# The two query tiles as one pair job ahead of the xg pair jobs, and wv tiles split by GpSimd with an accumulating DMA, in a one-core hybrid layer

## The chip, the cores and the metric

The kernel runs on 1 core of one Trainium2 chip (trn2). The metric is device time in microseconds (us), the median of several runs. The engines are named as in the profile: PE is TensorE's matmul and PEld its weight load, DVE is VectorE, ACT ScalarE, POOL GpSimd, SP SyncE, which here only issues DMAs.

## The reference

One layer of a streaming encoder, batch 1, 512 tokens (SEQ), width 1024 (D): a SwiGLU block, a mixing block, and a second SwiGLU block, each between two RMS norms. All is float32. The change lies in the mixing block:

```
u = pre_mix(h)
q, k, v, xr, xg = split(u @ w_in)            # 1024, 256, 256, 1024, 1024 columns
hr  = rg_lru(causal_conv(xr))                # gated linear recurrence over the tokens
y_a = (hr * gelu(xg)) @ w_lru_out
y_b = sliding_window_attention(q, k, v) @ w_attn_out     # 16 query heads of 64, 4 key/value heads
g   = sigmoid(u @ w_gate + b_gate)
h   = h + post_mix((g[:, :, 0] * y_a + g[:, :, 1] * y_b) @ w_o)
```

## The kernel before, in words

**Arithmetic.** Every product is made of three TensorE products in the format fp32r: a float32 operand w is split into a high half `whi` (w rounded to fp32r) and a low half `wlo` (w − whi, rounded), and x·w is taken as whi·xh + wlo·xh + whi·xl. The activations u are split once, into `uT`. Weight tiles (128 x 1024, 512 KB) arrive as float32 in slots named `raw_...`, are split on the way, and used once. A ring of 42 slots of 4 KB per partition (`NSLOT`) holds raw tiles, halves and intermediate results alike: an instruction that fills a slot waits for the last reader of what was in it.

**Who splits.** The high half comes from ScalarE (`act.activation`, Copy) or, for the tiles named in `BY_POOL`, from GpSimd; the low half is a VectorE subtraction (L179 for plain tiles). Tiles in `BY_DMA` are split without VectorE (`split_dma`, L154 to L162): ScalarE makes hi, ScalarE fills lo with −w rounded to fp32r, and a DMA issued by GpSimd adds w to it, so that w less its rounded value stays. Before the change `BY_DMA` holds two tiles of wg.

**Plain units.** `unit(nm, i)` is one tile of 128 output features: 8 blocks of the contraction times 3 matmuls of 128x512. `get` takes the split tile and sees to it that the next tiles of the list `order` are loaded and split ahead of time.

**Pair jobs.** Tiles named in `paired` are not split by `get`. Two of them (256 output features) form a job of class `Pairs`, which computes the 2x2 block product (two halves of the contraction by two tiles, two halves of the tokens) with seven products in place of eight (a Strassen-like scheme with Winograd's sums). Each product is `mm_s`: 4 blocks times 3 matmuls of 128x256, 12 in all, so a job has 84. The weight sums of job m are made in steps, `prep(m, 0)` to `prep(m, 4)`: step 0 makes S12 and S34 from the two raw tiles by four GpSimd additions of 128x512 (L538 to L544); steps 1, 2, 3 split the raw tile, S12 and S34 into halves (ScalarE L213, VectorE L214, 128x1024 each); step 4 splits a22 (128x512, named `w`). The sums on the side of u are the tiles t1 to t4 (`Xh`, `Xl`), which `later` spills to memory for use by another stage.

`GeluPairs.run` runs the four xg jobs. In each the products come in the order a11, s1, the previous job's a22 (`last`), s2, a12, s4, s3; ScalarE copies partial results out of PSUM into a tile `ct` (L658 to L694), VectorE adds them into `cc` (L671, L676, L683), ScalarE applies gelu (L650), VectorE multiplies by the recurrence's result (`mult`, L698) and the product is split (`parts`). The preparation of job n+1 stands inside job n.

**Order around the change.** Work of the mixing block runs on TensorE in this order: four xr units, eight wg units (gates), two wk units (keys), the four token tiles of V (L1236 to L1238, weights wv), two wq units (queries, tiles 0 and 1), the four xg jobs, then attention with the other wq units. Side work (convolution, the recurrence's gates and scans, the preparation of the first pair job, copies out of PSUM) is put into a queue by `later(n, fn, rank)`: it runs when `point()` has been called n more times. There are about two such calls to a unit; `point(True)` before the xg jobs runs whatever is left. The due points are tables at the end of the file: `PREP_AT` for the five steps of the first pair job, `PREP_1` for step 0 of the second, `RAW_AT` for the loading of their raw tiles. [...]

**Queries before.** `q_out` (L1244 to L1251) scales a wq unit's PSUM result into a tile `QS` whose lower 64 partitions hold the high half and the upper 64 the low one: two ScalarE copies (L1248) and two VectorE instructions (L1250) per tile.

Of the kernel before, what the change touches and what calls it, by code (L numbers as in the profile page):

```python
# [11 lines left out]
F32R = mybir.dt.float32r  # L12
AF = mybir.ActivationFunctionType
ALU = mybir.AluOpType

P = 128
SEQ = 512
D = 1024
# [6 lines left out]
HD = 64  # L25
# [26 lines left out]
def hybrid_layer(ctx: ExitStack, tc: tile.TileContext, a: dict, out: bass.AP):  # L52
    nc = tc.nc
    act, dve, pool, pe, sp = nc.scalar, nc.vector, nc.gpsimd, nc.tensor, nc.sync
# [47 lines left out]
    order = []  # L102
# [4 lines left out]
    paired = set()  # L107
# [11 lines left out]
    order += [("xr", i) for i in range(8)]  # L119
    order += [("wg", i) for i in range(8)]  # L120
    order += [("wk", 0), ("wk", 1), ("wv", 0), ("wv", 1)]
    order += [("wq", 0), ("wq", 1)]
    paired.update(range(len(order), len(order) + 8))
    order += [("xg", i) for i in range(8)]

    att_units = [("wq", 2), ("lru", 0), ("wq", 3), ("lru", 1), ("wq", 4), ("wq", 5), ("lru", 2), ("lru", 3)]
    att_units += [("wq", 6), ("lru", 4), ("wq", 7), ("lru", 5), ("lru", 6), ("lru", 7)]
# [9 lines left out]
    st = {"dma": 0, "split": 0, "get": 0}  # L137
    raws, pairs = {}, {}
# [10 lines left out]
    def dma_to(n):  # L149
        while st["dma"] < min(n, len(order)):  # L150
            dma_one(st["dma"])
            st["dma"] += 1

    def split_dma(r, src, shape=(P, D), hi=None):  # L154

        lo = slot(list(shape), F32R, name="wlo")
        if hi is None:
            hi = slot(list(shape), F32R, name="whi")
            act.activation(hi, r, AF.Copy)
        act.activation(lo, r, AF.Copy, scale=-1.0)  # L160
        pool.dma_start(out=lo, in_=src, accum_op=ALU.add)
        return hi, lo  # L162

    def split_to(n):
        while st["split"] < min(n, len(order)) and st["split"] not in paired:
            k = st["split"]
            dma_to(k + 1)
            r = raws.pop(k)
            if order[k] in BY_DMA:
                nm, i = order[k]  # L170
                pairs[k] = split_dma(r, a[nm][i * P : (i + 1) * P, :])
            else:
                hi = slot([P, D], F32R, name="whi")
                lo = slot([P, D], F32R, name="wlo")
                if order[k] in BY_POOL:
                    pool.tensor_copy(hi, r)
                else:
                    act.activation(hi, r, AF.Copy)
                dve.tensor_tensor(out=lo, in0=r, in1=f32(hi), op=ALU.subtract)  # L179
                pairs[k] = (hi, lo)  # L180
            st["split"] += 1

    def get(nm, i, ahead=2, rawahead=3):

# [12 lines left out]
    def later(n, fn, rank=1):  # L197
        uid[0] += 1
        due.append((now[0] + n, rank, uid[0], fn))
# [29 lines left out]
    def unit(nm, i, **kw):  # L229
        w = get(nm, i)  # L230
        ps = bank("f")
        mm_feat(ps, w, **kw)
        return ps
# [251 lines left out]
    def mm_s(wa, x, ps, more=False, mark=True):  # L485

        wh, wl = wa
        for k in range(4):
            s = slice(k * P, (k + 1) * P)
            xh, xl = x(0, k), x(1, k)  # L490
            first = k == 0 and not more
            pe.matmul(ps, wh[:, s], xh, start=first, stop=False, skip_group_check=True)  # L492
            pe.matmul(ps, wl[:, s], xh, start=False, stop=False, skip_group_check=True)  # L493
            pe.matmul(ps, wh[:, s], xl, start=False, stop=k == 3, skip_group_check=True)  # L494
        if mark:
            point()
# [144 lines left out]
    class GeluPairs(Pairs):  # L641


        def run(self, scans, yh, yl, tail, between):
            X, end = self.X, len(self.jobs) - 1
            assert st["get"] == st["split"] == self.k0, (st, self.k0)
            st["get"] = st["split"] = self.k0 + 2 * len(self.jobs)
            self.raws(2)
            last = mult = parts = lambda: None
            gelu = lambda v: act.activation(v, v, AF.Gelu_apprx_tanh)  # L650
            for n, (nm, f) in enumerate(self.jobs):
                W = self.w.pop(n)
                tmp = slot([P, 4, 256], name="ct")
                q1, q5, u, v = (tmp[:, i, :] for i in range(4))
                c = slot([P, 2, SEQ], name="cc")
                bu, bx, bc = (bank("c")[:, :256] for _ in range(3))
                mm_s(W["a11"], X["b11"], bu)
                act.activation(q1, bu, AF.Copy)  # L658
                mm_s(W["s1"], X["t1"], bx)
                act.activation(q5, bx, AF.Copy)  # L660
                self.prep(n + 1, 1)
                between(n)
                last()
                mm_s(W["s2"], X["t2"], bu, True)
                act.activation(u, bu, AF.Copy)
                mult()
                self.prep(n + 1, 2)

                def c11():
                    mm_s(W["a12"], X["b21"], bc)  # L670
                    dve.tensor_tensor(out=c[:, 0, :256], in0=bc, in1=q1, op=ALU.add)  # L671

                if n < end:
                    c11()
                mm_s(W["s4"], X["b22"], bx, True)
                dve.tensor_tensor(out=c[:, 0, 256:], in0=bx, in1=u, op=ALU.add)  # L676
                parts()
                self.prep(n + 1, 3)
                if n == end:
                    tail()  # L680
                mm_s(W["s3"], X["t3"], bu, True)
                act.activation(v, bu, AF.Copy)
                dve.tensor_tensor(out=c[:, 1, 256:], in0=v, in1=q5, op=ALU.add)  # L683
                if n == end:
                    c11()
                gelu(c[:, 0, :])
                if n < end:
                    self.prep(n + 1, 4)
                    self.prep(n + 2, 0)
                self.raws(n + 3)  # L690

                def last(W=W, bu=bu, c=c):
                    mm_s(W["a22"], X["t4"], bu, True)
                    act.activation(c[:, 1, :256], bu, AF.Gelu_apprx_tanh)  # L694
                    gelu(c[:, 1, 256:])

                def mult(c=c, f=f):
                    dve.tensor_tensor(out=c, in0=c, in1=scans[f // 2], op=ALU.mult)  # L698

                def parts(c=c):  # L700
                    yh.append(slot([P, 2, SEQ], F32R, name="yh"))
                    yl.append(slot([P, 2, SEQ], F32R, name="yl"))
                    split2(yh[-1], yl[-1], c)

            tail()
            last()
            mult()
            parts()

# [118 lines left out]
    ps = [bank("f") for _ in range(NS)]  # L828
# [23 lines left out]
    xg, tg = {(hh, th): slot([P, 4, 256], name="xg") for hh in range(2) for th in range(2)}, {}  # L852
# [291 lines left out]

    X3 = {"b11": uview(0, 0), "b21": uview(1, 0), "b22": uview(1, 1)}
    pairs_g = GeluPairs(("xg",), 0, 8, X3)

    def t_hi(key, src):
        X3[key] = slot([P, 4, 256], F32R, name="Xh")
# [3 lines left out]
    t_parts = {}  # L1153

    def t_lo(key, src):
        t_parts[key] = split_dma(src, src, (P, 4, 256), X3[key])
        X3[key] = pair_view(t_parts[key])

    def t_spill(key):
        for e, x in enumerate(t_parts.pop(key)):  # L1160
            sp.dma_start(out=t_scr[2 * (int(key[1]) - 1) + e], in_=f32(x))
# [12 lines left out]
    for i, p in enumerate(PREP_AT):  # L1174
        later(p, lambda i=i: pairs_g.prep(0, i), 3)
    later(PREP_1, lambda: pairs_g.prep(1, 0), 3)
    for n, p in enumerate(RAW_AT):
        later(p, lambda n=n: [dma_one(pairs_g.k0 + 2 * n + j) for j in range(2)], 3)


    lru, scans = {}, []
# [19 lines left out]
    for i in range(8):  # L1201
        ps = unit("wg", i)
# [16 lines left out]
    for i in range(2):  # L1219
        ps = unit("wk", i)  # L1220
        later(1, lambda i=i, ps=ps: k_out(i, ps))
    wv = [get("wv", i) for i in range(2)]
# [6 lines left out]
    for t in range(NT):  # L1229
        ps = bank("v")  # L1230
        c = slice(t * P, (t + 1) * P)
# [10 lines left out]
    QS = {}  # L1242

    def q_out(i, ps):  # L1244
        q_ = slot([P, 2, SEQ], F32R, name="QS")
        sc = HD ** -0.5
        for j, r0 in ((0, 0), (1, 64)):
            act.activation(q_[0:64, j, :], ps[r0 : r0 + 64, :], AF.Copy, scale=sc)  # L1248
        for j, r0 in ((0, 0), (1, 64)):
            dve.scalar_tensor_tensor(out=q_[64:128, j, :], in0=ps[r0 : r0 + 64, :], scalar=sc, in1=f32(q_[0:64, j, :]), op0=ALU.mult, op1=ALU.subtract)  # L1250
        QS[i] = q_  # L1251

    for i in range(2):
        ps = unit("wq", i)
        later(1, lambda i=i, ps=ps: q_out(i, ps))

    yh, yl = [], []
    point(True)
    spills = {1: ("t1", "t2"), 2: ("t3", "t4")}
    pairs_g.run(scans, yh, yl, lambda: split_to(st["split"] + 1), lambda n: [t_spill(key) for key in spills.get(n, ())])  # L1260
    X3 = pairs_g = None

    def ya_out(i, ps):
# [126 lines left out]
    for nm, i in att_units:  # L1390
        w = w_first or get(nm, i)
        w_first = None
        ps = bank("f")
# [34 lines left out]
    for i in range(8):  # L1428
        if i:
            w = get("wao", i)  # L1430
        ps = bank("f")
# [42 lines left out]
SCAN_LAG = (1, 2, 3, 4, 5, 6, 7, 8)  # L1474

T_AT = (3, 4, 5, 6), (4, 5, 6, 7)
RAW_AT = (18, 27)
PREP_AT = (22, 27, 29, 31, 33)
PREP_1 = 30
NSLOT = 42  # L1480

WGP = 14
# [1 line left out]
GRAW_AT = (29, 30)  # L1484
TB_AT = (34, 35, 36, 37)

BY_DMA = {("wg", i) for i in range(2)}

BY_POOL = {("wg", i) for i in range(2, 8)} | {("wk", 0), ("wk", 1)}
RF = 7  # L1490
# [60 lines left out]
```

## Time and profile before

| | before |
|---|---|
| runs, us | 1128.3, 1129.07, 1129.15; median 1129.07 |
| the profiled execution's own time, us | 1128.54 |
| its span, us | 1126.8 |
| granted TensorE clock, mean | 0.998 |
| PE busy in the span, us | 1118.7 (99%) |
| DVE / ACT / POOL busy, us | 833.1 / 620.8 / 362.0 |
| V matmuls start | 462.10 |
| the two wq units start | 473.61 |
| the first xg job starts | 484.52 |

The times in the lower rows are microseconds from the span's start, and come from the timeline. In a timeline row the first number is the start, the second the duration, then engine, line, operation, output<-inputs, shape; in brackets stands how long the engine sat idle before it, and what ended that. Rows with an "x2" join two equal neighbours. In rows by source the three durations are minimum, median and maximum in ns.

### The profile page before, as it was taken

To read this page: it belongs to the slowest core of one execution; us is meant where nothing else is said; L and a number is where in the kernel's file an instruction comes from. 1 tells how busy PE (TensorE), PEld (TensorE's weight loads), DVE (VectorE), ACT (ScalarE), POOL (GpSimd) and SP (SyncE) were. 2 spreads that over 40 slices of the span, in tenths; PEclk is the share of its full clock that TensorE was granted. 3 is DMA by queue.
4 is the path that set the end of the run, shared out by engine and by line. 5 is a ranking of instruction groups with operands and counts; after the bars stand their busy time and mean duration, and the time that the engine had idled before them with its cause. 6 is when DMAs were issued, how large, how long until landed. Compare 5 with 4: busy or idle time off the path is not lost.

```text
span 1126.8 us, 18041 instructions
## 1 busy us (share of the span) xinstructions
PE 1118.7 (99%) x7018; PEld 1012.3 (90%) x7018; DVE 833.1 (74%) x1233; ACT 620.8 (55%) x1107; POOL 362.0 (32%) x282
## 2 busy tenths in 40 slices
PE   9999999999999999999999999999999999999997
PEld 8899999988889977899888888889999999998886
DVE  5889989886436998887778867767898777975313
ACT  7755555574325788756655654456555555564211
POOL 0044344200000523232656663000866566700000
PEclk9999999999999999999999999999999999999999
DMA  9226563265213553156132336521333232264101
GB/s 346 96 86 148 133 133 113 76 224 164 98 57 139 164 116 105 38 165 247 57 94 75 131 112 225 180 101 38 113 105 93 103 113 87 87 203 167 38 20 56
DMA packets 40310, 136.54 MB, mean 121 GB/s; under 512 B 4880, under 2 KB 6800, under 8 KB 40224
## 3 DMA queue, kind: packets, MB, share of 16 engines
q1 hardware_dynamic: 36432, 123.28, 32.4%
q0 software_dynamic: 3504, 11.58, 5.2%
q8 instruction: 55, 0.90, 0.3%
q10 hardware_dynamic: 288, 0.52, 0.1%
q14 instruction: 31, 0.25, 0.1%
HBM read 121.74 MB, written 11.53 MB: 118 GB/s over the span
## 4 chain that ended last, share of the span: by engine, by line
PE 99%; DVE 0%; issue 0%; DVEq 0%; POOL 0%; ACT 0%; POOLq 0%
PE c L492 13%; PE c L493 13%; PE c L494 13%; PE f L223 9%; PE f L224 9%; PE f L225 9%; PE acc L243 8%; PE acc L241 8%; PE acc L242 8%; PE pt L1329 1%; PE s L1293 1%; PE s L1292 1%; PE tr L333 1%; PE o L1345 1%; PE o L1346 1%; PE f L847 1%
## 5 line engine op out<-in xcount | busy, mean ns | idle before, releaser
L493 PE MATMUL c<-uT,wlo 128*128 128x256 f32 x516 | 146.0, 283 | 0.0
L494 PE MATMUL c<-uT,whi 128*128 128x256 f32 x516 | 146.0, 283 | 0.0
L492 PE MATMUL c<-uT,whi 128*128 128x256 f32 x516 | 146.0, 283 | 0.0
L493 PE MATMUL c<-Xh,wlo 128*128 128x256 f32 x504 | 142.7, 283 | 0.0
L492 PE MATMUL c<-Xh,whi 128*128 128x256 f32 x504 | 142.7, 283 | 0.0
L223 PE MATMUL f<-uT,whi 128*128 128x512 f32 (+1 forms) x392 | 140.6, 359 | 0.0
L224 PE MATMUL f<-uT,wlo 128*128 128x512 f32 (+1 forms) x392 | 139.1, 355 | 0.0
L225 PE MATMUL f<-uT,whi 128*128 128x512 f32 (+1 forms) x392 | 139.0, 355 | 0.0
L241 PE MATMUL acc<-whi,hT 128*128 128x512 f32 x352 | 137.1, 390 | 0.0
L242 PE MATMUL acc<-wlo,hT 128*128 128x512 f32 x352 | 137.0, 389 | 0.0
L243 PE MATMUL acc<-whi,hT 128*128 128x512 f32 x352 | 136.9, 389 | 0.0
L214 DVE TENSOR_TENSOR wlo<-S,whi 128x1024 fp32r<-128x1024 f32 x86 | 126.7, 1473 | 7.5 <-POOL OL L1365 4.5
L494 PE MATMUL c<-Xl,whi 128*128 128x256 f32 x456 | 129.0, 283 | 0.0
L213 ACT ACTIVATE whi<-S 128x1024 fp32r<-128x1024 f32 x86 | 88.3, 1054 | 23.7 <-DVE S L539 22.0
L493 PEld LDWEIGHTS c<-uT,wlo 128*128 128x128 f32 x516 | 99.0, 192 | 0.2
L492 PEld LDWEIGHTS c<-uT,whi 128*128 128x128 f32 x516 | 99.0, 192 | 0.2
L494 PEld LDWEIGHTS c<-uT,whi 128*128 128x128 f32 x516 | 99.0, 192 | 0.0
L492 PEld LDWEIGHTS c<-Xh,whi 128*128 128x128 f32 x504 | 96.8, 192 | 0.3 <-issue 0.3
L493 PEld LDWEIGHTS c<-Xh,wlo 128*128 128x128 f32 x504 | 96.7, 192 | 0.1
L494 PEld LDWEIGHTS c<-Xl,whi 128*128 128x128 f32 x456 | 87.5, 192 | 0.0
L223 PEld LDWEIGHTS f<-uT,whi 128*128 128x128 f32 x392 | 74.1, 189 | 11.6 <-issue 1.6
L225 PEld LDWEIGHTS f<-uT,whi 128*128 128x128 f32 x392 | 74.1, 189 | 10.5
(380 smaller groups left out, 2858.5 us busy)
## 6 DMA issues: line engine op xcount, KB each, us to landing
raw_w2a<-in_w2a_dram SPq DMA_DIRECT2D x22, 512.0 KB, 4.0
raw_w1b<-in_w1b_dram SPq DMA_DIRECT2D x22, 512.0 KB, 4.3
raw_w3b<-in_w3b_dram SPq DMA_DIRECT2D x22, 512.0 KB, 4.2
raw_w2b<-in_w2b_dram SPq DMA_DIRECT2D x22, 512.0 KB, 4.0
raw_w3a<-in_w3a_dram SPq DMA_DIRECT2D x21, 512.0 KB, 4.5
raw_w1a<-in_w1a_dram SPq DMA_DIRECT2D x20, 512.0 KB, 4.3
raw_wg<-in_wg_dram SPq DMA_DIRECT2D x16, 512.0 KB, 3.8
raw_xr<-in_xr_dram SPq DMA_DIRECT2D x8, 512.0 KB, 3.9
```

The lines of the kernel that those rows point to most:

```text
L213: act.activation(hi, src, AF.Copy)
L214: dve.tensor_tensor(out=lo, in0=src, in1=f32(hi), op=ALU.subtract)
L223: pe.matmul(ps[:, c0:c1], wh[:, s], h_, start=k == 0, stop=False)
L224: pe.matmul(ps[:, c0:c1], wl[:, s], h_, start=False, stop=False)
L225: pe.matmul(ps[:, c0:c1], wh[:, s], l_, start=False, stop=k == KT - 1)
L241: pe.matmul(acc[n], x[:, 0, c], wh[:, s], start=first, stop=False)
L242: pe.matmul(acc[n], x[:, 0, c], wl[:, s], start=False, stop=False)
L243: pe.matmul(acc[n], x[:, 1, c], wh[:, s], start=False, stop=last)
L333: pe.transpose(ps[:, k * P : (k + 1) * P], hg[:, kk * P : (kk + 1) * P], ident)
L492: pe.matmul(ps, wh[:, s], xh, start=first, stop=False, skip_group_check=True)
L493: pe.matmul(ps, wl[:, s], xh, start=False, stop=False, skip_group_check=True)
L494: pe.matmul(ps, wh[:, s], xl, start=False, stop=k == 3, skip_group_check=True)
```

## The change

1. The two wq tiles become job 0 of the object that runs the xg jobs, so that they are computed by 84 matmuls of 128x256 instead of 48 of 128x512. Every step of preparation moves: step 0 to 4 at points 20, 25, 27, 28, 30 (`PREP_AT`) are now those of the wq pair, `PREP_1` is the first xg pair, and the later pairs follow inside the jobs. The raw tiles are loaded two to three points earlier (`RAW_AT`), the spills of t1 to t4 one job later.
2. The output of the wq job goes to the new function `q_pair`, called for tile 0 at the place of `mult` and for tile 1 at the place of `parts` in the next job. It makes QS as `q_out` did (with the two halves swapped for the second head of a tile), but reads `cc` in SBUF, not PSUM.
3. The two wv tiles are split without ScalarE and VectorE: GpSimd copies hi, multiplies by −1 into lo, and issues the accumulating DMA. They are loaded at points 16 and 19 and split at points 20 and 23 (`V_AT`).

```diff
@@ order
     order += [("wk", 0), ("wk", 1), ("wv", 0), ("wv", 1)]
-    order += [("wq", 0), ("wq", 1)]
-    paired.update(range(len(order), len(order) + 8))
-    order += [("xg", i) for i in range(8)]
+    paired.update(range(len(order), len(order) + 10))
+    order += [("wq", 0), ("wq", 1)] + [("xg", i) for i in range(8)]
@@ split_dma, split_to
-    def split_dma(r, src, shape=(P, D), hi=None):
+    def split_dma(r, src, e=act, shape=(P, D), hi=None):
         lo = slot(list(shape), F32R, name="wlo")
         if hi is None:
             hi = slot(list(shape), F32R, name="whi")
-            act.activation(hi, r, AF.Copy)
-        act.activation(lo, r, AF.Copy, scale=-1.0)
+            if e is pool:
+                pool.tensor_copy(hi, r)
+            else:
+                act.activation(hi, r, AF.Copy)
+        if e is pool:
+            pool.tensor_scalar(out=lo, in0=r, scalar1=-1.0, scalar2=None, op0=ALU.mult)
+        else:
+            act.activation(lo, r, AF.Copy, scale=-1.0)
         pool.dma_start(out=lo, in_=src, accum_op=ALU.add)
...
-            dma_to(k + 1)
+            st["split"] += 1
+            split_one(k)
+
+    def split_one(k):
+        if k not in pairs:
+            dma_one(k)
             r = raws.pop(k)
             if order[k] in BY_DMA:
                 nm, i = order[k]
-                pairs[k] = split_dma(r, a[nm][i * P : (i + 1) * P, :])
+                pairs[k] = split_dma(r, a[nm][i * P : (i + 1) * P, :], act if nm == "wg" else pool)
...
@@ GeluPairs.run
-                gelu(c[:, 0, :])
+                if nm == "xg":
+                    gelu(c[:, 0, :])
...
-                def last(W=W, bu=bu, c=c):
+                def last(W=W, bu=bu, c=c, nm=nm):
                     mm_s(W["a22"], X["t4"], bu, True)
+                    if nm == "wq":
+                        act.activation(c[:, 1, :256], bu, AF.Copy)
+                        return
...
-                def mult(c=c, f=f):
+                def mult(c=c, f=f, nm=nm):
+                    if nm == "wq":
+                        q_pair(f, c[:, 0, :])
+                        return
...
-                def parts(c=c):
+                def parts(c=c, f=f, nm=nm):
+                    if nm == "wq":
+                        q_pair(f + 1, c[:, 1, :])
+                        return
...
     pairs_g = GeluPairs(("xg",), 0, 8, X3)
+    pairs_g.jobs.insert(0, ("wq", 0))
+    pairs_g.k0 -= 2
...
+    for i, p in enumerate(V_AT):
+        k = order.index(("wv", i))
+        later(p - 4, lambda k=k: dma_one(k), 3)
+        later(p, lambda k=k: split_one(k), 3)
...
-    for i in range(2):
-        ps = unit("wq", i)
-        later(1, lambda i=i, ps=ps: q_out(i, ps))
+    def q_pair(i, c):
+
+        q_ = slot([P, 2, SEQ], F32R, name="QS")
+        sc = HD ** -0.5
+        for j, r0 in ((0, 0), (1, 64)):
+            act.activation(q_[r0 : r0 + 64, j, :], c[r0 : r0 + 64, :], AF.Copy, scale=sc)
+        for j, r0 in ((0, 0), (1, 64)):
+            dve.scalar_tensor_tensor(
+                out=q_[64 - r0 : 128 - r0, j, :], in0=c[r0 : r0 + 64, :], scalar=sc, in1=f32(q_[r0 : r0 + 64, j, :]),
+                op0=ALU.mult, op1=ALU.subtract)
+        QS[i] = q_
...
-    spills = {1: ("t1", "t2"), 2: ("t3", "t4")}
+    spills = {2: ("t1", "t2"), 3: ("t3", "t4")}
...
-RAW_AT = (18, 27)
-PREP_AT = (22, 27, 29, 31, 33)
-PREP_1 = 30
+RAW_AT = (16, 24)
+PREP_AT = (20, 25, 27, 28, 30)
+PREP_1 = 27
+V_AT = (20, 23)
...
-BY_DMA = {("wg", i) for i in range(2)}
+BY_DMA = {(nm, i) for nm in ("wg", "wv") for i in range(2)}
```

More of the change, by code (lines that the diff above doesn't have):

```diff
@@ L180, in split_to @@
                 pairs[k] = (hi, lo)
-            st["split"] += 1
     def get(nm, i, ahead=2, rawahead=3):
@@ L641, in hybrid_layer, with run @@
     class GeluPairs(Pairs):
-        def run(self, scans, yh, yl, tail, between):
+        def run(self, scans, yh, yl, q_pair, tail, between):
             X, end = self.X, len(self.jobs) - 1
@@ L1155, in t_lo @@
     def t_lo(key, src):
-        t_parts[key] = split_dma(src, src, (P, 4, 256), X3[key])
+        t_parts[key] = split_dma(src, src, act, (P, 4, 256), X3[key])
         X3[key] = pair_view(t_parts[key])
@@ L1251, in q_out @@
         QS[i] = q_
-    for i in range(2):
-        ps = unit("wq", i)
-        later(1, lambda i=i, ps=ps: q_out(i, ps))
+    def q_pair(i, c):
[8 more added lines that the diff above has]
+        QS[i] = q_
     yh, yl = [], []
     point(True)
-    spills = {1: ("t1", "t2"), 2: ("t3", "t4")}
-    pairs_g.run(scans, yh, yl, lambda: split_to(st["split"] + 1), lambda n: [t_spill(key) for key in spills.get(n, ())])
+    spills = {2: ("t1", "t2"), 3: ("t3", "t4")}
+    pairs_g.run(scans, yh, yl, q_pair, lambda: split_to(st["split"] + 1), lambda n: [t_spill(key) for key in spills.get(n, ())])
     X3 = pairs_g = None
```

## The prediction

> **What bounds the kernel now.** The profile page comes first: span, busy engines, and the chain that ended last.
>
> ```profile
> span 1126.8 us, 18041 instructions
> PE 1118.7 (99%) x7018; PEld 1012.3 (90%) x7018; DVE 833.1 (74%) x1233; ACT 620.8 (55%) x1107; POOL 362.0 (32%) x282
> ...
> PE 99%; DVE 0%; issue 0%; DVEq 0%; POOL 0%; ACT 0%; POOLq 0%
> ```
>
> TensorE is the chain. The waits of TensorE show whether anybody holds it up:
>
> ```profile
> PE w L796 <- POOL warm L793: 1.1, 1, 1.1
> ```
>
> One wait, at the very start. So two things can move the time: how many TensorE microseconds there are, and whether the change makes TensorE wait where it never did. The 74% of VectorE is a mean over stages; the view by windows (us, then busy PE, PEld, DVE, ACT, POOL, then the granted clock, the DMA share, GB/s) gives the stages that the change touches: the two wq units, the first xg job, the stretch in which the last gates run, the stretch from there to the end of the units, and everything from the last long idle time of VectorE to the end of its split for the last xg job.
>
> ```profile
> 473.61:484.52 10.91, 10.91 (x50) 9.02 (x49) 10.78 (x13) 3.36 (x7) 2.54 (x2) 1.00 0.16 46
> 484.52:493.15 8.63, 8.63 (x73) 8.63 (x72) 6.58 (x9) 5.17 (x8) 2.55 (x2) 1.00 0.17 66
> 430.00:443.00 13.00, 13.00 (x63) 10.26 (x62) 12.10 (x13) 10.07 (x15) 6.99 (x5) 1.00 0.28 82
> 443.00:484.00 41.00, 41.00 (x227) 35.91 (x227) 35.68 (x41) 28.53 (x43) 7.68 (x6) 1.00 0.16 46
> 429.84:513.43 83.59, 83.59 (x533) 75.60 (x532) 73.42 (x77) 58.51 (x90) 28.71 (x18) 1.00 0.34 114
> ```
>
> TensorE is full in each at clock 1.00, but VectorE has 83.59 − 73.42 = 10.17 us free in the last row, 12%, of which 0.90 lie before 443 and so 9.27 after. ScalarE has 25 us free there. This is the stage to which the change adds work.
>
> **TensorE's part.** The two wq units are 48 matmuls of 512 columns, 10.91 us. A pair job issues 72 matmuls of 256 columns before the next one's first (its seventh product, 12 of its 84, goes into the next job): 8.63 / 72 = 0.120 us each, and 84 cost 10.07. The change saves 10.91 − 10.07 = 0.84 us. The span of the profiled execution lies 1.74 us below its 1128.54, which is 0.53 below the median of the runs, 1129.07. With everything else hidden the profiled execution would become 1128.54 − 0.84 = 1127.70. No more can come out, as TensorE waits nowhere else.
>
> **VectorE's price for GpSimd's work.** First the rows of VectorE with nobody beside it:
>
> ```profile
> 446.34 0.69 DVE L1128 SCALAR_TENSOR_TENSOR xc_t<-xc_t 128x512 f32<-128x512 f32 x1
> 480.37 1.22 DVE L214 TENSOR_TENSOR wlo<-S,whi 128x1024 fp32r<-128x1024 f32 x1
> 516.62 0.68 DVE L214 TENSOR_TENSOR w<-raw_xg,w 128x512 fp32r<-128x512 f32 x1
> 523.38 0.42 DVE L683 TENSOR_TENSOR cc<-ct 128x256 f32<-128x256 f32 x1
> ```
>
> And the same forms while GpSimd makes the sums S of an xg pair (four additions of 128x512 per pair); first and last row of the four batches of before, and then a cast on GpSimd beside a VectorE instruction:
>
> ```profile
> 436.99 1.28 POOL L543 TENSOR_TENSOR S<-raw_xg 128x512 f32<-128x512 f32 x1 [2.76 <-PE r L1112]
> 437.08 1.75 DVE L1128 SCALAR_TENSOR_TENSOR xc_t<-xc_t 128x512 f32<-128x512 f32 x1
> 442.55 1.11 DVE L1097 SCALAR_TENSOR_TENSOR ig<-ig,xc_t 128x512 f32<-128x512 f32 x1 [0.59 <-ACT ig L1096]
> 473.42 1.58 DVE L214 TENSOR_TENSOR wlo<-S,whi 128x1024 fp32r<-128x1024 f32 x1 [0.66 <-ACT whi L213]
> 474.92 1.79 DVE L1139 TENSOR_TENSOR ig<-xc_t,ig 128x512 f32<-128x512 f32 x1
> 492.33 1.53 DVE L214 TENSOR_TENSOR wlo<-S,whi 128x1024 fp32r<-128x1024 f32 x1
> 497.73 1.51 DVE L214 TENSOR_TENSOR wlo<-raw_xg,whi 128x1024 fp32r<-128x1024 f32 x1 [0.73 <-ACT whi L213]
> 503.47 2.32 DVE L214 TENSOR_TENSOR wlo<-S,whi 128x1024 fp32r<-128x1024 f32 x1
> 509.01 2.15 DVE L214 TENSOR_TENSOR wlo<-raw_xg,whi 128x1024 fp32r<-128x1024 f32 x1
> 433.10 1.14 POOL L176 CAST whi<-raw_wk 128x1024 fp32r<-128x1024 f32 x1 [7.50 <-PE f L224]
> 433.44 1.34 DVE L1128 SCALAR_TENSOR_TENSOR xc_t<-xc_t 128x512 f32<-128x512 f32 x1
> ```
>
> 0.69 became 1.75 at 437.08, 1.22 became 2.32 at 503.47: a VectorE instruction with two operands in SBUF waits for the GpSimd instruction that runs. Summed over a batch (duration less the undisturbed one) the loss is 3.53 us in the first (4 instructions), 1.47 in the second (2), 1.76 in the third (4), 4.22 in the fourth (4): 11.0 in all, 2.75 on average. The first and fourth met a VectorE without idle time: 3.9 on average. A cast cost 1.34 − 0.69 = 0.65. [...]
>
> **What VectorE loses and gets of its own.** Removed:
>
> ```profile
> 453.47 1.23 DVE L179 TENSOR_TENSOR wlo<-raw_wv,whi 128x1024 fp32r<-128x1024 f32 x1 [1.13 <-ACT whi L178]
> 458.32 1.20 DVE L179 TENSOR_TENSOR wlo<-raw_wv,whi 128x1024 fp32r<-128x1024 f32 x1
> 467.46 2.33 DVE L179 TENSOR_TENSOR wlo<-raw_wq,whi 128x1024 fp32r<-128x1024 f32 x2
> 484.39 1.39 DVE L1250 SCALAR_TENSOR_TENSOR QS<-f,QS 64x512 fp32r<-64x512 f32 x2
> 485.95 1.39 DVE L1250 SCALAR_TENSOR_TENSOR QS<-f,QS 64x512 fp32r<-64x512 f32 x2 [0.17 <-ACT QS L1248]
> ```
>
> 1.23 + 1.20 + 2.33 + 2.78 = 7.54 us. Added for the wq pair: three splits of 128x1024 (3 x 1.22) and one of 128x512 (0.68), three additions into cc (3 x 0.42), four of q_pair (4 x 0.69): 8.36 us. Net +0.82. q_pair's four also read both operands from SBUF now, where L1250 read one from PSUM, so they can be held up too.
>
> **GpSimd.** It gets a fifth batch of S, and for each wv tile a cast, a multiplication by −1 and the issue of an accumulating DMA. No row shows this multiplication; the nearest:
>
> ```profile
> L1313 POOL TENSOR_SCALAR P<-P,d x64: 593/921/1963, 537.0 to 663.4; 128x256 f32<-128x256 f32 x48, 128x128 f32<-128x128 f32 x16
> L161 POOL DMA_DIRECT2D wlo<-in_wg_dram x2: 869/879/889, 383.8 to 394.6; - x2
> DMA to landing us min/median/max: 4.7/5.7/9.2
> ```
>
> The same operation takes 0.593 at 128 columns and 0.921 at 256, so by the line through both, an estimate, 0.593 + 7 x 0.328 = 2.89 at 1024; the cast of this shape took 1.14. As a cast loses VectorE about 0.5 less than its duration (1.14 against 0.65), a multiplication costs it between 0.6 and 2.4. I take 2.0, nearer the row of the same operation, and a little below as that one also reads a column of scalars. [...]
>
> **The sum, to VectorE's split of S12 for the last xg job.** The deadline:
>
> ```profile
> 512.22 1.21 DVE L214 TENSOR_TENSOR wlo<-S,whi 128x1024 fp32r<-128x1024 f32 x1
> 514.87 0.28 PE L493 MATMUL c<-Xh,wlo 128*128 128x256 f32 x1
> 463.53 0.28 PE L1236 MATMUL v<-whi,uT 128*128 128x256 f32 x1
> ```
>
> The split ends at 513.43, 1.44 us before TensorE needs it. Lateness: own work +0.82; deadline earlier +0.84; S batches, five at 3.9 against 11.0, +8.5 (VectorE will have no idle time in any; from 2.75 each to 4.22 each: +2.75 to +10.1); wv on GpSimd, two casts at 0.65 and two multiplications at 2.0, +5.3 (2.5 to 6.1). Together 15.46. Against it: the margin 1.44 and the idle time 9.27, all of it eaten. Left: 15.46 − 10.71 = 4.75 us, which TensorE waits: 1127.70 + 4.7 = **1132.4 us**. It won't wait in one place: VectorE's splits come an engine queue's order behind one another, so a late one shows at the second product of the wq job (s1, then s2), and again in xg jobs 1 to 3.
>
> Low end: 0.82 + 0.84 + 2.75 + 2.5 = 6.9, below 10.71, all hidden: 1127.7. High end: 17.9 less 10.71 gives 7.2, so 1134.9; and 3 more if a third of the idle time can't be used, since it stands where VectorE waits for ScalarE's high half: 1138.
>
> **Other parts, cover and prices.** ScalarE: loses the high halves of two wv and two wq tiles, gets three and a half such halves and five copies out of PSUM at 0.38 (next row); q_pair has as many copies as q_out; about +1.5 us against 25 free. What stands in its queue matters more:
>
> ```profile
> 505.88 0.38 ACT L658 ACTIVATE ct<-c 128x256 f32<-128x256 f32 x1 [1.02 <-DVE wlo L214]
> ```
>
> The copy q1 into a new ct tile waited 1.02 us for VectorE's split to free the slot. Behind q1 stand q5 and the next high half; the product s2 writes the bank that q1 must have read. In the wq job and the next three, this wait gets longer by what VectorE is late: the place where lateness reaches TensorE first.
>
> GpSimd's queue: S of the wq pair, cast, multiplication and DMA of wv0 stand ahead of the casts of wk0 and wk1, then those of wv1, then S of the first xg pair. From 433: four sums at 1.46 ((6.99 − 1.14) / 4 by the row 430 to 443), 1.1 + 2.0 to 2.9 + 0.87, two casts at 1.1 and 1.5, again 1.1 + 2.0 to 2.9 + 0.87, come to 449.5 to 451.5, and the DMA lands 5.7 (up to 9.2) later: 455 to 461. TensorE needs wv1 at 463.53 (the first 12 of the V matmuls use wv0). So 2.5 to 8 us of cover; if it is gone, each us late is a us of the time. SyncE: the raw tiles of wq and wv are loaded some points earlier and the spills of t1 to t4 run one job later, beside a DMA share of 0.16 in the row 443 to 484; cost nothing, the same transfers. The attention uses the QS of tiles 0 and 1 after three more jobs: nothing.
>
> **The rivals.**
> *Everything is hidden* (the other side: not slower). If the multiplication costs the 0.6 of a cast's row and the five batches the mean 2.75 or little more, the sum of 6.9 to 10 fits in the 10.71 and TensorE never waits: 1127.7. It decides as long as the added lateness stays under 10.71. For it: the second and third batch cost only 1.5 to 1.8. Against: they were cheap because VectorE waited for ScalarE there, which is the idle time that is spent already. [...]
> *GpSimd's own chain is late*: V waits for wv1's DMA, or wk0's split for its cast. From the bounds above it decides if GpSimd starts wv0 over 3 to 8 us later than 439 (a slot not free, a raw tile not landed). Price: some 3 us on top, 1135.4.
> [...]
> *The change doesn't do what it says*, or TensorE gets faster by something that I don't see: the built program has 36 more matmuls (84 for 48), as said, so little is left here.
>
> **How the numbers follow.** What a measurement of this kernel can tell from no change is about 0.2%, 2.3 us: 1126.8 to 1131.3. The forecast, VectorE late in the pair jobs, has 0.60, with a range of its own of 1130.5 to 1136.5; 0.08 of it lies below 1131.3. Everything hidden 0.19. GpSimd's chain late 0.13. Whole batches 0.05. The rest 0.03. So same 0.19 + 0.08 = 0.27; slower 0.52 + 0.13 + 0.05 = 0.70; faster 0.03. The range reaches from the hidden case to most of the late ones: 1127.6 to 1138.
>
> **What the profile after would show.** Right: TensorE busy some 0.8 us less, and waits of 4 to 6 us in all on lines of the pair products (mm_s), put down to VectorE's wlo or ScalarE's copies; VectorE idle under 3 us from 443 to the last xg job; the multiplication on GpSimd above 1.5 us, and VectorE's neighbours of it stretched by as much. First matmul of the wq job at 473.6 as before. Wrong: no waits of TensorE there (hidden); waits at L1236 or in the wk units (GpSimd's chain); a multiplication at 1.1 us; or VectorE instructions stretched by several GpSimd instructions in a row.

## The result, and the profile after

| | before | after |
|---|---|---|
| median of 5 runs, us | 1128.73 (1128.05 to 1129.15) | 1139.27 (1137.76 to 1139.81) |
| ratio to before | | 1.0091, 95% interval 1.0076 to 1.0105 |
| profiled execution, us | 1128.54 | 1137.76 |
| its span, us | 1126.8 | 1135.9 |

Slower by 10.5 us, where 3.3 were forecast and 1138.0 was the upper end of the range. The profiled execution is the fastest of the five, so the accounts below are made against its own +9.1 us of span.

The page of after, the same lines as of before, and the view of TensorE's waits (line of the waiting instruction, who released it, us in total, times, longest):

```profile
span 1135.9 us, 18147 instructions
...
PE 1121.2 (99%) x7054; PEld 1016.1 (89%) x7054; DVE 844.3 (74%) x1236; ACT 622.4 (55%) x1112; POOL 378.9 (33%) x292
...
PE 93%; DVE 2%; issue 1%; POOL 1%; ACT 1%; DMA 0%; DVEq 0%; SPq 0%; POOLq 0%; ACTq 0%
```

```profile
PE c L501 <- ACT ct L667: 6.3, 2, 3.4
PE w L815 <- POOL warm L812: 1.1, 1, 1.1
PE f L232 <- DVE o L1393: 0.3, 1, 0.3
```

Two things are new. TensorE waits 6.3 us at two places. And it is *busy* 2.5 us longer, 1121.2 against 1118.7, though the change takes 0.84 us of work from it. The timeline of TensorE at the first place, and its row at the second:

```profile
479.79 0.39 PE L501 MATMUL c<-Xh,whi 128*128 128x256 f32 x1 [3.44 <-ACT ct L667]
480.01 0.28 PE L502 MATMUL c<-Xh,wlo 128*128 128x256 f32 x1
...
480.61 0.37 PE L501 MATMUL c<-Xh,whi 128*128 128x256 f32 x1
480.78 0.42 PE L502 MATMUL c<-Xh,wlo 128*128 128x256 f32 x1
480.99 0.42 PE L503 MATMUL c<-wlo,whi 128*128 128x256 f32 x1
...
504.56 0.58 PE L501 MATMUL c<-Xh,whi 128*128 128x256 f32 x1 [2.86 <-ACT ct L667]
```

Both waits are those of the product s2 (into the bank that the copy q1, L667, must have read): in the wq job, and in the third job. The matmuls behind start 0.12 us apart at first, and 0.21 apart from 480.78 on. The view by windows says why (us, then busy PE, PEld, DVE, ACT, POOL, then the granted clock):

```profile
479.00:482.00 3.00, 2.21 (x13) 2.21 (x14) 2.93 (x6) 1.96 (x5) 0.00 (x0) 0.78 0.20 70
482.00:484.00 2.00, 2.00 (x12) 2.00 (x11) 1.99 (x3) 1.33 (x2) 0.00 (x0) 0.50 0.47 176
484.00:486.00 2.00, 2.00 (x18) 2.00 (x18) 1.98 (x3) 0.66 (x1) 0.00 (x0) 0.98 0.28 27
504.56:507.94 3.38, 3.38 (x16) 3.38 (x17) 2.86 (x4) 2.27 (x6) 0.60 (x1) 0.50 0.97 388
443.00:484.00 41.00, 37.56 (x227) 34.12 (x226) 33.54 (x36) 26.15 (x41) 16.16 (x11) 0.96 0.31 78
484.00:524.00 40.00, 37.14 (x296) 36.94 (x296) 38.97 (x36) 25.36 (x42) 20.68 (x12) 0.96 0.53 176
```

After each of the two waits the clock is granted at 0.50 for about 3.4 us, in which TensorE does half the work: some 1.65 us lost each time. By the busy time the two cost 1121.2 − (1118.7 − 0.84) = 3.3 us. So +9.1 = 6.3 (waits) + 3.3 (half clock) − 0.84 (fewer matmuls) + 0.3 (the wait at L232).

Who was late? Rows of POOL, DVE and ACT, from the timelines of after, for the first wait and then for the second:

```profile
441.17 3.21 POOL L163 TENSOR_SCALAR wlo<-raw_wv 128x1024 fp32r<-128x1024 f32 x1
446.68 3.01 DVE L189 TENSOR_TENSOR wlo<-raw_wk,whi 128x1024 fp32r<-128x1024 f32 x1 [2.57 <-POOL whi L186]
475.51 1.41 DVE L1238 TENSOR_TENSOR KS<-f,KS 64x512 fp32r<-64x512 f32 x2
476.23 1.35 ACT L1241 ACTIVATE KS<-KS 64x512 fp32r<-64x512 f32 x2 [3.46 <-DVE KS L1238]
478.83 0.64 ACT L222 ACTIVATE V<-v 128x256 fp32r<-128x256 f32 x2
479.35 0.39 ACT L667 ACTIVATE ct<-c 128x256 f32<-128x256 f32 x1
...
498.85 2.99 DVE L1285 SCALAR_TENSOR_TENSOR QS<-cc,QS 64x512 fp32r<-64x512 f32 x2
501.86 2.17 DVE L223 TENSOR_TENSOR wlo<-S,whi 128x1024 fp32r<-128x1024 f32 x1
504.12 0.38 ACT L667 ACTIVATE ct<-c 128x256 f32<-128x256 f32 x1 [3.40 <-issue]
```

First: TensorE needs the bank at 476.35 (479.79 less its wait of 3.44). ScalarE reaches q1 at 479.35, behind the copies of V, behind the copies of KS, which waited 3.46 us for VectorE's KS of the second wk unit at 475.51. In the kernel before the same two instructions stand 5.7 us earlier:

```profile
469.82 1.41 DVE L1213 TENSOR_TENSOR KS<-f,KS 64x512 fp32r<-64x512 f32 x2
470.54 1.36 ACT L1216 ACTIVATE KS<-KS 64x512 fp32r<-64x512 f32 x2 [3.63 <-DVE KS L1213]
```

And there the two wq units gave the copies behind them 10.9 us more of TensorE's time. So two things came together: VectorE was late for KS, and the cover was gone. Second: q1 of the third job starts at 504.12. The row names no releaser; by the times it waits for its slot, which VectorE's split of S34 gives back at 504.03 (501.86 + 2.17). Ahead of that split stand two q_pair instructions that took 2.99 us beside GpSimd's sums.

### The profile page after: what moved, and what is told of

Its sections match the earlier page's. It is cut to its first block, busy times and chain, and to the rows that moved or that the text cites. A ratio compares the mean times of both kernels' runs of the same rounds, so it can differ in the third digit from the quotient of the medians.

```text
span 1135.9 us, 18147 instructions
## 1 busy us (share of the span) xinstructions
PE 1121.2 (99%) x7054; PEld 1016.1 (89%) x7054; DVE 844.3 (74%) x1236; ACT 622.4 (55%) x1112; POOL 378.9 (33%) x292
## 4 chain that ended last, share of the span: by engine, by line
PE 93%; DVE 2%; issue 1%; POOL 1%; ACT 1%; DMA 0%; DVEq 0%; SPq 0%; POOLq 0%; ACTq 0%
PE c L501 13%; PE c L502 13%; PE c L503 13%; PE acc L250 8%; PE acc L251 8%; PE acc L252 8%; PE f L232 8%; PE f L233 8%; PE f L234 8%; PE pt L1362 1%; PE s L1326 1%; PE tr L342 1%; PE s L1325 1%; PE f L866 1%; PE o L1379 1%
## 5 line engine op out<-in xcount | busy, mean ns | idle before, releaser
L501 PE MATMUL c<-Xh,whi 128*128 128x256 f32 x516 | 147.1, 285 | 6.3 <-ACT ct L667 6.3
L501 PE MATMUL c<-uT,whi 128*128 128x256 f32 x528 | 150.1, 284 | 0.0
L502 PE MATMUL c<-uT,wlo 128*128 128x256 f32 x528 | 150.0, 284 | 0.0
L503 PE MATMUL c<-uT,whi 128*128 128x256 f32 x528 | 149.9, 284 | 0.0
L502 PE MATMUL c<-Xh,wlo 128*128 128x256 f32 x516 | 146.9, 285 | 0.0
L223 DVE TENSOR_TENSOR wlo<-S,whi 128x1024 fp32r<-128x1024 f32 x88 | 129.9, 1476 | 7.0 <-POOL OL L1398 3.1
L232 PE MATMUL f<-uT,whi 128*128 128x512 f32 (+1 forms) x376 | 134.4, 357 | 0.3 <-DVE o L1393 0.3
L233 PE MATMUL f<-uT,wlo 128*128 128x512 f32 (+1 forms) x376 | 132.8, 353 | 0.0
L234 PE MATMUL f<-uT,whi 128*128 128x512 f32 (+1 forms) x376 | 132.8, 353 | 0.0
L501 PEld LDWEIGHTS c<-uT,whi 128*128 128x128 f32 x528 | 102.1, 193 | 0.1
L503 PEld LDWEIGHTS c<-uT,whi 128*128 128x128 f32 x528 | 101.9, 193 | 0.0
L502 PEld LDWEIGHTS c<-Xh,wlo 128*128 128x128 f32 x516 | 99.8, 193 | 0.1
L232 PEld LDWEIGHTS f<-uT,whi 128*128 128x128 f32 x376 | 71.1, 189 | 11.5 <-issue 1.4
L234 PEld LDWEIGHTS f<-uT,whi 128*128 128x128 f32 x376 | 71.1, 189 | 9.8
```

What stands on the lines that cost most here:

```text
L223: dve.tensor_tensor(out=lo, in0=src, in1=f32(hi), op=ALU.subtract)
L232: pe.matmul(ps[:, c0:c1], wh[:, s], h_, start=k == 0, stop=False)
L233: pe.matmul(ps[:, c0:c1], wl[:, s], h_, start=False, stop=False)
L234: pe.matmul(ps[:, c0:c1], wh[:, s], l_, start=False, stop=k == KT - 1)
```

## The experiments

All kernels below were timed beside the kernel before; the time of `waits` is that of a single execution. **Theory A**: two waits with separate causes of order. **Theory B**, the sum on record: VectorE and GpSimd have too much to do in all.

**pair_only.** `V_AT` stays, wv is split by ScalarE and VectorE.

```diff
-BY_DMA = {(nm, i) for nm in ("wg", "wv") for i in range(2)}
+BY_DMA = {("wg", i) for i in range(2)}
```

> Edit: the wq pair job as changed, but the two wv tiles split by ScalarE and VectorE at the same points 20 and 23. Theory A (two waits, each with its own cause: the first because the cast of wk0 stands in GpSimd's queue behind the 3.2 us multiplication of wv0, so that VectorE idles 2.6 us and is late for KS, the second because the four q_pair instructions delay VectorE's split of S34 and with it the slot of ct): the first wait shrinks from 3.4 to 1 us or less and its half-clock stretch goes, the second stays at 2.9 us with its half clock: 1128.7 - 0.8 + 1 + 2.9 + 1.6 = about 1133.4. Theory B (the sum on record: VectorE and GpSimd together have too much to do, and any work taken away counts wherever it stands): wv's cost on VectorE falls by about 6 us of contention less 2.4 of its own work, so about 1135.5, and both waits shrink alike.

Measured 1137.45 us, ratio 1.0080 (1.0067 to 1.0092); TensorE's rows:

```profile
479.30 0.39 PE L501 MATMUL c<-Xh,whi 128*128 128x256 f32 x1 [2.91 <-ACT ct L667]
...
504.08 0.58 PE L501 MATMUL c<-Xh,whi 128*128 128x256 f32 x1 [2.87 <-ACT ct L667]
```

Both theories are wrong here: nearly the whole loss is still there. Splitting wv on GpSimd accounts for 1.8 us of the 10.5 by the medians and 0.3 by the profiled spans; the intervals overlap, so the 2.9 that the sum had (5.3 less VectorE's own 2.4) isn't excluded by the times alone. The waits say more: the sum would leave 4.75 − 2.9 = 1.9 us of them, and 5.8 are there. The first wait does not come from the cast of wk0 behind a multiplication, as A had it: that 2.57 us of idle time is gone, and the wait shrank by only 0.5.

**wv_only.** The kernel before with the third part of the change alone: `split_dma` with GpSimd for wv, at `V_AT = (20, 23)`; wq stays two units.

```diff
+    for i, p in enumerate(V_AT):
+        k = order.index(("wv", i))
+        later(p - 4, lambda k=k: dma_one(k), 3)
+        later(p, lambda k=k: split_one(k), 3)
...
-BY_DMA = {("wg", i) for i in range(2)}
+BY_DMA = {(nm, i) for nm in ("wg", "wv") for i in range(2)}
```

> Edit: the kernel before with nothing but the two wv tiles split by GpSimd at points 20 and 23; wq stays two units. Theory A: the wq units are 11 us in which ScalarE and VectorE catch up, the first wait can't arise and q_pair isn't there: no wait, 1128.7, same. Theory B: about 6 us of contention less 2.4 of removed work against 9.3 of idle time and 1.4 of margin: hidden too, 1128.7. Rival C (GpSimd's chain is late for V): a wait at the V products of 1 to 3 us, 1130 to 1132.

Measured 1128.31 us, ratio 0.9998 (0.9990 to 1.0007), no wait at V or in the wk units. wv on GpSimd costs nothing that can be measured where the wq units follow, and rival C falls.

**wv_early.**

```diff
-V_AT = (20, 23)
+V_AT = (10, 12)
```

> Edit: the changed kernel with the wv tiles split by GpSimd at points 10 and 12 in place of 20 and 23, ahead of the sums of the wq pair; no work is taken away. Theory A: the cast of wk0 no longer waits behind a multiplication, the first wait and its half clock go (3.4 + 1.6), the second shrinks to 1 to 2.1 us (no half clock if it is short enough): 1130 to 1132. Theory B: the same work, the same time within 1 us, 1138 to 1140.

Measured 1134.50 us, ratio 1.0055 (1.0043 to 1.0068):

```profile
478.18 0.38 ACT L667 ACTIVATE ct<-c 128x256 f32<-128x256 f32 x1 [1.85 <-DVE w L223]
...
478.61 0.39 PE L501 MATMUL c<-Xh,whi 128*128 128x256 f32 x1 [2.18 <-ACT ct L667]
...
502.25 0.39 PE L501 MATMUL c<-Xh,whi 128*128 128x256 f32 x1 [1.75 <-ACT ct L667]
```

With the same work 4.8 us came back by the medians (2.4 by the profiled spans), which B as stated excludes; but A's first wait did not go. What holds q1 up is now another thing: ScalarE is through with KS and V at 476.33, and q1 waits 1.85 us more for VectorE's split of a22, which stands behind KS, V and a scan in VectorE's queue. The edit also moves wv's part (multiplications at 398.7 and 408.5) ahead of the stretch that the sum counts, which begins at 429.84. So it doesn't test the sum itself.

**q_late.** Both `q_pair` calls move from job 1 to job 3, ahead of its product s3.

```diff
                 parts()
                 self.prep(n + 1, 3)
+                if n == 3:
+                    q_pair(0, held[0][:, 0, :])
+                if n == 3:
+                    q_pair(1, held[0][:, 1, :])
...
-                        q_pair(f, c[:, 0, :])
...
-                        q_pair(f + 1, c[:, 1, :])
+                        held.append(c)
```

> Edit: the changed kernel with both q_pair calls moved from job 1 into job 3 (counted from 0, the wq job); wv as changed. Theory A: the second wait goes with its half clock (2.9 + 1.6), the first stays at 3.4 with its half clock: 1139.3 - 4.5 = about 1134.8, with a short wait in job 3 possible. Theory B: the four instructions only move within the stage, and the deadline for the last xg split lies behind them still: 1138 to 1140.

Measured 1134.84 us, ratio 1.0057 (1.0043 to 1.0071). The second wait is gone, the first unchanged, and a short one is new, released by the copy v of job 3, which stands behind the four q_pair copies:

```profile
PE c L501 <- ACT ct L668: 3.4, 1, 3.4
PE c L501 <- ACT ct L696: 1.2, 1, 1.2
```

The second wait went, as A had it. That the time met A's 1134.8 is in part luck: A's figure left the new wait out, and by the profiled spans 3.1 us came back, not 4.5. The calls now stand behind the deadline that the sum uses (VectorE's split of S12 for the last xg job ends at 517.73, the first of the four starts at 520.70), not ahead of it as was expected, so this run doesn't separate A from the sum either.

**filled.** Is the half clock a price of its own? The change with dummy matmuls in place of the waits:

```diff
+                for _ in range({0: 28, 2: 24}.get(n, 0)):
+                    pe.matmul(bc, W["a11"][0][:, :P], X["b11"](0, 0), start=True, stop=True)
                 mm_s(W["s2"], X["t2"], bu, True)
```

> Edit: the changed kernel with matmuls whose product is never read in the place of the two waits: 28 of 128x256 (3.4 us) ahead of the product s2 of the wq job and 24 (2.9 us) ahead of that of job 2. Theory D (the half clock after each long wait is a price of its own, 1.6 us each): TensorE never idles long, the clock stays at 1.00 and the time falls by up to 3.2 us, to about 1136. Theory E (VectorE is late anyway, and TensorE at half speed only takes away waits that would come next): the time stays within 1 us of 1139, with new waits of 1 to 2 us in jobs 1 to 3.

Measured 1137.04 us, ratio 1.0079 (1.0065 to 1.0093), no wait at the two places. Between D and E: 2.2 us less than after by the medians (0.6 by the two profiled spans), and this came up in job 1:

```profile
487.37 0.38 PE L502 MATMUL c<-uT,wlo 128*128 128x256 f32 x1 [1.55 <-DVE wlo L223]
489.60 0.39 PE L502 MATMUL c<-Xh,wlo 128*128 128x256 f32 x1 [0.53 <-DVE wlo L223]
```

At full clock 2.1 us of waits come next that the half clock had taken away, so of its 3.3 us about 1.2 were its own price. By the times this price is 0.6 to 2.2 us, and the interval overlaps that of after, so its size isn't settled.

**waits.** How long a wait halves the clock? The kernel before with four waits of rising length in the gate units.

```diff
+        if i in {1: 1, 3: 3, 5: 5, 7: 8}:
+            psz = bank("w")
+            pe.matmul(psz[:, :256], zt[:, :P], zt, start=True, stop=True)
+            for _ in range({1: 1, 3: 3, 5: 5, 7: 8}[i]):
+                pool.memset(f32(zt), 0.0)
+            pe.matmul(psz[:, :256], zt[:, :P], zt, start=True, stop=True)
         ps = unit("wg", i)
```

> Edit: the kernel before with four waits of TensorE of growing length put ahead of the gate units 1, 3, 5 and 7: a matmul into an unused bank waits for 1, 3, 5 or 8 fills of a small tile by GpSimd, estimated at 0.5, 1.3, 2.0 and 3.1 us by the fills of the profile (0.30 us for 64x256). From the runs so far: no half clock after a wait of 1.22 us, half clock for 3.4 us after 1.75 us and more. Expected: none after the first, half clock after the third and fourth; the second tells where between the two the limit lies. [...]

The second to fourth wait in TensorE's timeline:

```profile
422.88 0.39 PE L1209 MATMUL w<-zt 128*128 128x256 f32 x1 [1.51 <-POOL zt L1208]
438.36 0.39 PE L1209 MATMUL w<-zt 128*128 128x256 f32 x1 [2.24 <-POOL zt L1208]
456.23 0.58 PE L1209 MATMUL w<-zt 128*128 128x256 f32 x1 [3.03 <-POOL zt L1208]
```

And the 3.38 us behind each, by windows:

```profile
422.88:426.26 3.38, 3.38 (x15) 2.60 (x17) 2.38 (x3) 0.00 (x0) 1.92 (x2) 1.00 0.71 285
438.36:441.74 3.38, 3.38 (x10) 2.73 (x11) 2.41 (x2) 0.00 (x0) 2.22 (x3) 0.60 0.13 53
456.23:459.61 3.38, 3.38 (x9) 2.73 (x10) 2.31 (x3) 2.83 (x6) 0.93 (x1) 0.51 0.00 0
```

Full clock after 1.51 us, half after 2.24 and 3.03. Its time was 1140.61; its span is 12.0 us longer than that of before: 7.2 of waits, and TensorE busy 4.8 us more, of which some 3 by half clock. The rest, extra matmuls and their issue, was not taken apart.

**early_late.** wv_early and q_late together.

> Edit: the changed kernel with wv split by GpSimd at points 10 and 12 and both q_pair calls in job 3, the two edits that each took a part of the waits away. If the waits have separate causes: the second goes (1.75 + 1.6 of wv_early), the first stays at 2.2 us with its half clock: 1134.5 - 3.4 = about 1131. If the causes are one total of work: 1134 or more, as either edit alone.

Measured 1132.69 us (1130.76 to 1133.63), ratio 1.0039 (1.0026 to 1.0051). The second wait is gone, the first is there as in wv_early, 2.17 us; 0.5 us is left in job 4. The time lies between what the two readings expected; by the waits the causes are separate, as one is gone and the other untouched.

**spread.** The first wait by order alone, on top of early_late:

```diff
-    point(True)
+    point()
...
-SCAN_LAG = (1, 2, 3, 4, 5, 6, 7, 8)
+SCAN_LAG = (3, 4, 5, 6, 7, 8, 11, 12)
-PREP_AT = (20, 25, 27, 28, 30)
-PREP_1 = 27
+PREP_AT = (20, 23, 24, 25, 26)
+PREP_1 = 31
```

> Edit: as early_late, and VectorE's order ahead of the wq job changed so that its preparation comes first: steps 1 to 4 at points 23 to 26 in place of 25 to 30, the sums of the first xg pair at 31 in place of 27, each scan two to four points later (the last two fall into the pair jobs). No work is taken away. If both waits are questions of order: no wait in the pair jobs, the clock stays at 1.00, and the 84 for 48 matmuls are left: 1128.5 - 0.8 = 1127.7. If VectorE and GpSimd together have too much to do in the stage: waits of 2 us or more somewhere in jobs 0 to 4, 1131 or more.

Measured 1130.01 us, ratio 1.0017 (1.0008 to 1.0026). The first wait is gone. One is left in the pair jobs, at the copy v of job 3, whose queue holds four q_pair copies; in TensorE's timeline it is

```profile
516.94 0.38 PE L501 MATMUL c<-Xh,w 128*128 128x256 f32 x1 [1.57 <-ACT ct L696]
```

and the window behind it shows that it leaves the clock whole:

```profile
516.94:520.32 3.38, 3.38 (x28) 3.38 (x29) 3.29 (x6) 2.68 (x7) 0.00 (x0) 1.00 0.21 40
```

**spread_q34** puts one q_pair behind the copy v of job 3 and one behind that of job 4; **spread_q44** both behind that of job 4; **spread_plain_wv** is spread_q34 with `BY_DMA` as in pair_only, wv split by ScalarE and VectorE.

```diff
@@ spread_q34 (spread_q44: n == 4 in both)
                 dve.tensor_tensor(out=c[:, 1, 256:], in0=v, in1=q5, op=ALU.add)
                 if n == end:
                     c11()
+                if n == 3:
+                    q_pair(0, held[0][:, 0, :])
+                if n == 4:
+                    q_pair(1, held[0][:, 1, :])
```

> Edit: as spread, but the two q_pair calls stand behind the copy v of job 3 and of job 4, one each, where spread had both ahead of the copy of job 3. In spread the one wait left, 1.57 us, stood behind four q_pair copies of ScalarE (2.58 us) that ran ahead of that copy. If order alone decides: no wait in the pair jobs, 1128.3 - 0.8 = 1127.5, faster by 0.07%. If the stage has too much work in all: the wait of 1.5 us comes up elsewhere, 1129 to 1130 as spread.

> Edit: as spread_q34, with both q_pair calls behind the copy v of the last job (4). If order alone decides: 1127.5; the danger is at the start of attention, which reads QS soon after: a wait there of up to 2 us, 1129. If the stage has too much work in all: 1129 to 1130.

> Edit: as spread_q34, but the two wv tiles are split by ScalarE and VectorE, as in the kernel before, at points 10 and 12. If the change's third part (wv by GpSimd) is what makes room for the pair job, VectorE is late again by its 2.4 us and ScalarE by 2.1: a wait of 1 to 3 us, 1129 to 1132. If it makes no room, as what GpSimd does holds VectorE up by about as much: the same as spread_q34 within 0.5 us, 1127.5 to 1128.

| | median, us | ratio to before |
|---|---|---|
| spread_q34 | 1128.53 | 1.0001 (0.9992 to 1.0010) |
| spread_q44 | 1129.57 | 1.0011 (1.0002 to 1.0020) |
| spread_plain_wv | 1129.09 | 1.0007 (0.9999 to 1.0016) |

All waits of TensorE in spread_q34:

```profile
PE w L819 <- POOL warm L816: 1.1, 1, 1.1
PE f L232 <- DVE o L1397: 0.6, 1, 0.6
```

The two windows of the stage:

```profile
443.00:484.00 41.00, 41.00 (x270) 37.76 (x269) 34.45 (x42) 28.46 (x45) 10.20 (x7) 1.00 0.22 65
484.00:524.00 40.00, 39.85 (x332) 39.65 (x332) 39.17 (x37) 27.55 (x47) 22.03 (x15) 1.00 0.59 194
```

No wait in the pair jobs and no half clock, and no work was taken away. But this isn't order within the stage alone. Take the stretch that the forecast's sum counts, from VectorE's last long idle time to the end of its split of S12 for the last xg job, by the view of windows:

| | from, to | length, us | VectorE busy | VectorE idle |
|---|---|---|---|---|
| before | 429.84, 513.43 | 83.59 | 73.42 | 10.17 |
| after | 429.54, 522.09 | 92.55 | 83.75 | 8.80 |
| early_late | 429.64, 515.88 | 86.24 | 72.68 | 13.56 |
| spread_q34 | 429.48, 512.91 | 83.43 | 73.26 | 10.17 |
| spread_plain_wv | 429.86, 513.13 | 83.27 | 76.07 | 7.20 |

Moving wv ahead of this stretch and q_pair behind its end takes some 11 us of VectorE's busy time out of it (early_late). That leaves a wait of 2.17 us, though VectorE has less to do there than in the kernel before. The edits of spread then change the order of what is issued inside it: the wait goes, with as much VectorE work as in the kernel before, and in spread_plain_wv with 2.65 us more. So what early_late leaves of the first wait is a matter of order. Which of the edits in spread did it was not separated.

The 0.84 us doesn't show: the profiled span of spread_q34 is 1126.5 against 1126.8, with 0.6 us given back in attention at L232. spread_q44 has no wait in the pair jobs either, but 1.0 us at L232. wv on GpSimd makes no room that can be measured: the intervals of spread_plain_wv and spread_q34 overlap.

## Why the prediction was wrong, by its own steps

- **TensorE's saving: right.** In spread_q34 the wq job's first matmul is at 473.25 and the next job's at 481.89: 8.64 us for 72, where 8.63 was worked out.
- **A wait priced at its own length: a step that failed.** The sum took the clock to be 1.00 throughout, as in every row of before that it shows. After the waits of 1.75 us and more it was 0.50 for some 3.4 us (480.65 to 484.06 in after). That term, 3.3 us in the profiled execution, has no place in the prediction, and is more than the 1.3 us by which the median missed the range. Not all of it is extra: by filled, 2.1 us of it would have been waits at full clock.
- **Idle time taken as credit: the step that failed most.** 4.75 us of waits were forecast; 6.3 came, and at full clock it would have been some 8.4 (with the 2.1 of filled). The added work was not the error on the short side: in the forecast's stretch VectorE is busy 10.3 us more (83.75 against 73.42), where the sum had 14.6 (0.82, 8.5 and 5.3). But the sum set 9.27 us of VectorE's idle time against it, all eaten, and of the 10.17 us in the stretch 8.80 are still idle after. VectorE idles 41 − 33.54 = 7.46 us in 443 to 484 (5.32 before) and 1.03 in 484 to 524, where under 3 in all was named as the sign of being right. Of the 7.46 us VectorE waited 4.3 for ScalarE and 2.6 for GpSimd; that time wasn't there to be filled by an ordered queue. A total of work against a total of idle time at the last deadline was the wrong form of account: the deadline missed first was q1's, in the wq job, at the other end of the stage, and early_late misses it with less work for VectorE than the kernel before has.
- **Places: right; causes: one of two.** The second product of the wq job and a copy into ct that waits for VectorE's split were both named. The second wait is of that kind. At the first, q1 of the wq job stood in ScalarE's queue behind the copies of KS and V, which the prediction doesn't have. Job 1 had no wait: as filled shows, the half clock hid 2.1 us there.
- **S batches: right.** The stretch over the five batches of after adds up, instruction by instruction, to about 18.8 us; 19.5 was forecast. Not only instructions with two operands were held up: a tensor_scalar of VectorE with one (0.43 alone) took 1.39 at 434.97 beside the sums. Nor did each wait for whatever GpSimd ran: beside the multiplication at 441.17 two with two operands, from 442.83 on, took 1.28 together (0.69 each alone). The sums of before bear the step out: splits of 128x1024 end 1.09 us behind the end of the sum that ran beside them (493.86 against 492.77, 505.79 against 504.70), while two additions that read PSUM stayed at 0.42 and 0.41 (491.65 and 492.00, beside the sum at 490.52).
- **wv on GpSimd: the operation a little dearer than estimated, its effect on VectorE smaller.** The multiplication took 3.21 and 3.32 us in after, where the line through the rows gave 2.89; the cast of the same shape ahead of each took 1.50 and 1.33. But each held VectorE up by about 0.7 us (0.43 became 1.14 at 441.77, 0.69 became 1.34 at 450.40), where 2.0 was taken, and the neighbours were not stretched by as much as the multiplication lasts. Putting wv back is worth at most 1.8 us by the medians of pair_only, and 0 in wv_only.
- **Rivals.** Everything hidden is what spread_q34 shows could have been, not what this order gives. GpSimd's chain was not late for V: no wait there in any run. Whole batches, which the chances give 0.05, no run shows: beside the sums of after an instruction of VectorE took at most 1.11 us longer than alone (1.80 against 0.69 at 433.13, 2.32 against 1.21 at 512.12), where one sum takes 1.29 to 2.27. What came was the forecast's own case, with idle time that couldn't be used and with the half clock missing.

## What to carry to other kernels

Where a unit that needs little preparation stands ahead of one that needs much, it is cover: before moving or shrinking it, follow the first product that needs something from the side engines, through each engine's queue, rather than set the sum of their work against the sum of their idle time. Where TensorE waits 1.75 us or more, the least that halved the clock here, add the half clock behind the wait, 1.7 us at most (3.4 us at 0.50), and look whether it hides waits that would follow. When the side work is issued was worth ten microseconds here; the 0.84 us of the change itself can't be told from noise.

## What the runs showed of the hardware that was not expected

The clock of TensorE stayed at 1.00 after waits of 0.43 and 1.51 us (waits), 1.22 (q_late), 1.55 (filled) and 1.57 (spread). It fell to 0.50 after waits of 1.75 and 2.18 us (wv_early), 2.17 (early_late), 2.24 and 3.03 (waits), 2.86 and 3.44 (after), for some 3.4 us however long the wait had been: from 480.65 to 484.06 behind the 3.44 us of after, from 503.32 to 506.72 behind the 1.75 us of wv_early.

Its start kept no fixed distance from the end of the wait. In after it came 0.86 us behind the restart at 479.79 and 0.02 us ahead of the one at 504.56, in wv_early 1.07 us behind the one at 502.25; in pair_only the clock was at 0.50 from the restart at 504.08 on, to 506.92. What sets the start no run shows. The waits differ in place as well as in length, and no run varies one alone, so the limit between 1.57 and 1.75 us holds for these runs alone.

A GpSimd tensor_scalar of 128x1024 from float32 to fp32r took 3.21 and 3.32 us in after, more than twice the cast of that shape just ahead of each (1.50 and 1.33).
